# Second half of a two-layer backbone on five token blocks of one column group each, in place of four of two groups

## The chip, the cores and the metric

The kernel runs on one core of a Trainium2 chip. The metric is the device time of one execution in microseconds; the kernel before takes 1913.91 us (median of three runs, 1911.35 to 1915.99). The engines are named as in the profile: PE (TensorE, matrix products), ACT (ScalarE), DVE (VectorE), POOL (GpSimd), and SP, whose queue issues every data transfer (DMA) of this kernel in program order.

## The reference

One step of a two-layer network on 128 prompt tokens and 2048 latent tokens, 2176 in all, with 1024 channels. Layer 0 joins gated linear attention with a spatial gating unit; layer 1 joins a pooling mixer with a short gated convolution. The part that the change touches:

```python
def mix_odd(z, j):                       # layer 1; z = h @ w_in_odd, six parts of 512 channels
    xc, gc, xd, bd, cd, gd = split_cols(z, ODD_SPLITS)
    pooled = concat([centred_mean(xc[..., group i], w) for i, w in enumerate((2, 4, 8, 16))]) - xc
    pooled = einsum('btgc,gcd->btgd', pooled by group, w_pool[j])
    o_c = pooled * pool_scale[j] * silu(gc)
    u = cd * xd
    y = u[t-1] * w_conv[j, 0] + u[t] * w_conv[j, 1] + u[t+1] * w_conv[j, 2]
    return concat([o_c, bd * y * silu(gd)])
# each layer: h = rmsnorm(x) * (1 + scale) + shift;  out = mix(h @ w_in) @ w_out;  x = x + gate * out
# after both layers: y = rmsnorm(x, final_norm_g)
```

## The kernel before, in words

Channels lie on the 128 partitions and tokens along the free axis. Every fp32 product is made of three reduced-precision ones: an operand is split into a high and a low part (`split`, lines 197 to 199: the high part on ACT, the low part on DVE, every third one on POOL), and the product is hi·hi + hi·lo + lo·hi. With 8 contraction tiles of 128 that is 24 matmuls for one tile of 128 output channels and one column group.

The first half of the program is the in-projection of layer 0 with its attention and gating unit. It works on blocks of its own (`BLK`) and its tables are the same in both kernels. The second half works on the token blocks `BLK2`, from the last tokens to the first, because the backward attention state arrives in that order. For each block there are 40 output-channel tiles: 8 of `out0` (out-projection of layer 0), 24 of `in1` (in-projection of layer 1, four heads of six), and 8 of `out1` (out-projection of layer 1). The blocks are interleaved: out0 of the last two blocks, and then, for each block, its in1 and out1 and the out0 of the block two before it. The last block has only in1 and out1 (`out1_last`) left.

`gemm_ch` makes one output-channel tile. It loads the weights anew for every block (`load_w`: one DMA of 512 KB at line 206 into one of `NRAW = 2` raw buffers, then the split into one of three hi and three lo buffers), and runs 24 matmuls for each column group:

```python
for a, b in _groups(c1 - c0):
    pt = gtile()
    o = pt[:, 0:b - a]
    mm3(o, [...])          # 24 matmuls, line 217
    yield a, b, o
tick()
```

`_groups` keeps up to 512 columns in one group and halves what is wider, so a block of 544 gives two groups of 272. A raw weight buffer is free for the next DMA when the low part has been made from it.

Between two blocks the normed input h of in1 is made by `make_t` (line 350) and `make_h` (lines 365 and 366) from x, which is read back tile by tile through two `xk` buffers (line 1018). The tiles of h lie in the same ring as the outputs `ys` of out1, which have to be scaled (line 1126) and stored (line 1128) first; the norm for that is a side thread that runs two channel tiles later (`after(fin, 2)`). For block 1 alone `ys` lies in the `oB` buffers, which out0 of block 0 has just used (the loads into them are line 954). The attention's backward part (`finish_o`, lines 830 to 890) is another side thread, advanced by `tick`. The order of instructions on each engine is fixed when the program is built.

Of the kernel before, what the change touches and what calls it, by code (L numbers as in the profile page):

```python
# [10 lines left out]
F32 = mybir.dt.float32  # L11
# [14 lines left out]
# token ranges of the blocks of layer 0's in-projection; the prompt comes last  # L26
# [3 lines left out]
BLK2 = [(0, 544), (544, 1088), (1088, 1632), (1632, 2176)]  # L30
# [4 lines left out]
W2 = 552  # L35
TMAX = 600
# [44 lines left out]
def kernel(ctx: ExitStack, tc: tile.TileContext, xT, cT, w_ada, b_ada, norm_g, final_g,  # L81
# [33 lines left out]
    def mtile():  # L115
        """two psum banks"""
        return ps.tile([P, 2, 512], F32, tag="m", bufs=banks[0])
# [19 lines left out]
    # side threads: generators advanced as the main line of matrix products is emitted  # L137
# [82 lines left out]
    def gemm_ch(src, acts, c0, c1):  # L220
        """One tile of 128 output channels over columns [c0, c1) of the 8 (hi, lo) operand tiles.
        Yields (a, b, psum) per column group, relative to c0."""
# [12 lines left out]
    def newton(ss, scale, shape, nw=None):  # L235
        """ss (psum, sums of squares) -> (m, r0) with 1/sqrt(ss*scale + eps) = (m + 1.5) * r0."""
# [40 lines left out]
    def silu_psum(src, n, eng, pre=None, dst=None):  # L277
        """psum [P, n] -> SBUF silu; pre: per-partition factor."""
# [25 lines left out]
    def adaln(l, part, wtile, step, halves=(0, 2)):  # L304
        """shift (part 0), scale (1) or gate (2) of layer l for both conditionings, in channels
        [512 * halves[0], 512 * halves[1])."""
# [32 lines left out]
    def cond_ranges(t0, t1):  # L339
        """(a, b, cond) pieces, relative to t0, of tokens [t0, t1)."""  # L340
        out = []
        if t0 < NP:
            out.append((0, min(t1, NP) - t0, 0))
        if t1 > NP:
            out.append((max(t0, NP) - t0, t1 - t0, 1))
        return out
# [33 lines left out]
    # ================= phase 1: layer 0 in-projection, GLA within tiles, SGU =================  # L380
    sg = pool("sg", stack=s1)

    def cols(bi):
        """(column, token, count) of the pieces of block bi"""
        c = 0
        for a, b in BLK[bi]:
            yield c, a, b - a
            c += b - a
# [4 lines left out]
    def prep_x(bi, rr=None):  # L393
        """loads block bi of x and scales it by its norm"""
# [55 lines left out]
    # [hi, 1, 1 | lo | hi] of the low-rank gates against [hi, bias hi, bias lo | hi | lo] of w_gk  # L450
# [22 lines left out]
    def diag_ap(Z, arr, s):  # L473
        """[p, half, block, s]: array arr on first halves, array arr + 1 on second halves."""
# [5 lines left out]
    def gla_tile(t, qk, v, lrT):  # L480
        """GLA of tile t (0: prompt): within the tile in both directions, forward state, and what
        the backward sweep needs."""
# [6 lines left out]
        Z = gl.tile([P, 4, 256], F32, tag="Z", bufs=2)     # Sb, Pf, Sf, Pb  # L489
# [7 lines left out]
        Q1 = gl.tile([P, 2, 2, P], F32, tag="Q1", bufs=2)   # q, level-1 q  # L497
# [6 lines left out]
        while s <= 64:  # L504
# [10 lines left out]
            # advance the prefix and suffix sums to blocks of 2s  # L515
# [10 lines left out]
            if s == 8:  # L526
                # levels of blocks up to 16: 32x32 products, masked and summed
# [26 lines left out]
        # upper levels, laid out as the tile's matrix  # L554
# [23 lines left out]
        # whole-tile factors: backward q, forward q, forward k, backward k  # L578
# [16 lines left out]
        # k factors to token-major, chunk states  # L595
# [6 lines left out]
        # outputs of the tile  # L602
# [36 lines left out]
    def gemm_tok(src, ncol, h, nt):  # L639
        """Token-major: yields (tile, psum[tok, ncol]) for nt tiles of 128 tokens."""  # L640
# [22 lines left out]
    def first_units(h, nt, tok0, qk0):  # L663
        """lr | v and the first products of q, by halves of the contraction, the first half as soon
        as its part of h is there"""
# [16 lines left out]
    def block1(bi):  # L682
# [51 lines left out]
        # spatial gating unit: token-major values, mixed over the 128 positions of a tile  # L734
# [43 lines left out]
    # ================= backward sweep of GLA, norm and gate =================  # L778
# [7 lines left out]
    def open_late():  # L786
# [3 lines left out]
        f3.append(fin_o(3, 1, PER3))  # L790
# [8 lines left out]
    def heads(ap):  # L799
        """[(r k), pr, c] of DRAM as [k, pr, r, c]"""  # L800
# [10 lines left out]
    def states(t):  # L811
        """states entering tile t: [forward | backward, k] x head x v"""
# [16 lines left out]
    def finish_o(bi):  # L829
        """adds the backward state's part, norm and gate of GLA; operands of out-projection 0"""  # L830
# [61 lines left out]
    def fin_o(bi, every, per=1):  # L892
        """finish_o as a side thread; the operands are complete when `out` runs"""
# [38 lines left out]
    # ================= layer 0 out-projection, layer 1 =================  # L932
# [7 lines left out]
    width[:] = [TMAX, 560, 7, 2]  # L940
# [6 lines left out]
    def out_proj(l, t0, t1, o8, res, ytile, done, part=None):  # L947
        """res(c) + gate * (o @ w_out)[c] to done(c, .); returns the sum of squares over channels,
        or calls part with that of all channels but the last, for each column group of the last"""
# [17 lines left out]
    def out0(bi, o8):  # L967
# [6 lines left out]
        def fin():  # L974
            r = tmp.tile([P, 560], F32, tag="r2", bufs=1)[:, 0:n]
# [7 lines left out]
    def range1(bi):  # L983
        """tokens whose layer-1 output block bi makes"""
# [9 lines left out]
    def in1(bi):  # L994
        """layer-1 in-projection and branches; yields after each channel group, then the operands"""
# [17 lines left out]
        r = tmp.tile([P, 560], F32, tag="r", bufs=1)[:, 0:w]  # L1013
# [281 lines left out]
```

## Time and profile before

| | |
|---|---|
| median of three runs | 1913.91 us |
| span of the profiled execution, first to last instruction | 1907.3 us |
| what lies around the span (median less span) | 6.6 us |
| PE busy | 1800.5 us, 94% |
| DVE, ACT, POOL busy | 60%, 45%, 38% |
| second half | from about 859 us to the end |

The profile shows one execution. "x24" is a count of instructions, "idle before" is the time that an engine stood still ahead of them, with what ended it. In a row of matmuls the duration of one is longer than the distance to the next, because they are pipelined: what a matmul costs is read from the distance of the start times. PEclk is the granted clock of TensorE, 1.00 at 2.4 GHz and 0.5 at 1.2 GHz.

### The profile page before, as it was taken

What the parts mean: (1) busy time and instruction counts of PE and PEld (TensorE: products, weight loads), DVE (VectorE), ACT (ScalarE), POOL (GpSimd) and SP (SyncE); (2) the same over time, 40 slices, a digit from 0 to 9 for tenths busy, and PEclk for the clock granted to TensorE, in tenths of its full rate; (3) what the DMA queues carried; (4) which work ended last, traced back from release to release, by engine and by line L of the source; (5) the groups of instructions that cost most, each with busy time, mean ns of one, the idle gap of its engine ahead of it and who ended that gap; (6) DMA issues with size and microseconds to landing.
All of it is one profiled execution on the core that took longest, in us unless ns stands there. A gap on an engine that the chain in (4) does not pass through costs nothing. (4 is left out here: it accounts for less than half of the span.)

```text
span 1907.3 us, 40156 instructions
## 1 busy us (share of the span) xinstructions
PE 1800.5 (94%) x16303; PEld 1673.9 (88%) x16303; DVE 1150.2 (60%) x2069; ACT 858.5 (45%) x1678; POOL 725.4 (38%) x707
## 2 busy tenths in 40 slices
PE   5998899989998999988999999999999999999996
PEld 4886787777787898888899999999999999999996
DVE  5477835875489359766757554775535644636344
ACT  4454645455455356443535442354433433433332
POOL 0423532444153223453534533344533423442343
PEclk9999999999999999998999999999999999999998
DMA  9343424343523342455764343753245622343221
GB/s 321 114 137 117 162 90 151 122 147 119 170 90 113 109 136 81 129 160 170 243 211 156 113 134 114 235 165 111 84 136 177 214 89 89 115 136 128 85 86 63
DMA packets 136122, 263.44 MB, mean 138 GB/s; under 512 B 24192, under 2 KB 60160, under 8 KB 135936
## 3 DMA queue, kind: packets, MB, share of 16 engines
q1 hardware_dynamic: 135936, 260.87, 42.2%
q8 instruction: 128, 2.10, 0.4%
q14 instruction: 58, 0.48, 0.1%
HBM read 219.97 MB, written 40.84 MB: 137 GB/s over the span
## 5 line engine op out<-in xcount | busy, mean ns | idle before, releaser
L217 PE MATMUL ps_g<-ring_hh,wp_hi 128*128 128x272 f32 (+5 forms) x2168 | 679.0, 313 | 9.3 <-DVE tmp_ev L765 5.6
L217 PE MATMUL ps_g<-ring_hh,wp_lo 128*128 128x272 f32 (+5 forms) x2168 | 673.4, 311 | 0.2 <-POOL wp_lo L199 0.2
L217 PE MATMUL ps_g<-ring_hl,wp_hi 128*128 128x272 f32 (+5 forms) x2168 | 671.7, 310 | 1.7 <-DVE ring_hl L366 1.7
L198 ACT ACTIVATE wp_hi<-wp_raw 128x1024 fp32r<-128x1024 f32 (+1 forms) x256 | 270.9, 1059 | 426.3 <-PE ps_g L217 297.1
L217 PEld LDWEIGHTS ps_g<-ring_hh,wp_hi 128*128 128x128 f32 x2168 | 409.7, 189 | 32.7 <-DVE tmp_ev L765 6.6
L217 PEld LDWEIGHTS ps_g<-ring_hl,wp_hi 128*128 128x128 f32 x2168 | 410.2, 189 | 18.3 <-DVE ring_hl L366 2.3
L217 PEld LDWEIGHTS ps_g<-ring_hh,wp_lo 128*128 128x128 f32 x2168 | 409.6, 189 | 16.5 <-POOL wp_lo L199 0.3
L199 DVE TENSOR_TENSOR wp_lo<-wp_raw,wp_hi 128x1024 fp32r<-128x1024 f32 (+1 forms) x175 | 229.5, 1313 | 213.7 <-ACT wp_hi L198 213.2
L199 POOL TENSOR_TENSOR wp_lo<-wp_raw,wp_hi 128x1024 fp32r<-128x1024 f32 (+1 forms) x81 | 198.6, 2452 | 373.5 <-ACT wp_hi L198 373.2
L270 POOL TENSOR_TENSOR tmp_acc<-tmp_acc,tmp_px 128x544 f32<-128x544 f32 (+4 forms) x76 | 120.4, 1584 | 165.7 <-ACT tmp_px L269 162.8
L217 PE MATMUL ps_g<-wp_hi,ring_hh 128*128 128x256 f32 (+1 forms) x528 | 156.1, 298 | 15.0 <-ACT gl_v L700 4.2
L217 PE MATMUL ps_g<-wp_lo,ring_hh 128*128 128x256 f32 (+1 forms) x528 | 152.6, 290 | 1.8 <-POOL wp_lo L199 1.1
L217 PE MATMUL ps_g<-wp_hi,ring_hl 128*128 128x256 f32 (+1 forms) x528 | 152.0, 290 | 1.8 <-DVE ring_hl L366 1.7
L217 PE MATMUL ps_g<-oA_oh,wp_hi 128*128 128x272 f32 (+1 forms) x512 | 148.8, 295 | 4.9 <-ACT oA_oh L198 3.7
L217 PE MATMUL ps_g<-oA_ol,wp_hi 128*128 128x272 f32 (+1 forms) x512 | 149.4, 293 | 2.2 <-DVE oA_ol L199 2.0
L217 PE MATMUL ps_g<-oA_oh,wp_lo 128*128 128x272 f32 (+1 forms) x512 | 149.5, 293 | 0.5 <-DVE wp_lo L199 0.5
L217 PE MATMUL ps_g<-oB_ol,wp_hi 128*128 128x272 f32 (+1 forms) x512 | 147.4, 288 | 1.4 <-POOL oB_ol L199 1.4
L524 POOL TENSOR_TENSOR gl_Z<-gl_Z 128x128 f32<-128x128 f32 x170 | 89.8, 548 | 151.9 <-DVE gl_Z L524 110.5
L217 PE MATMUL ps_g<-oB_oh,wp_hi 128*128 128x272 f32 (+1 forms) x512 | 147.1, 289 | 0.4 <-ACT oB_oh L198 0.4
L217 PE MATMUL ps_g<-oB_oh,wp_lo 128*128 128x272 f32 (+1 forms) x512 | 147.5, 289 | 0.0
L508 ACT ACTIVATE gl_L<-gl_Z 128x256 f32<-128x256 f32 x204 | 82.1, 418 | 90.3 <-DVE gl_Z L524 60.5
L217 PEld LDWEIGHTS ps_g<-wp_hi,ring_hh 128*128 128x128 f32 x528 | 100.5, 191 | 23.0 <-ACT gl_v L700 4.9
(241 smaller groups left out, 3162.6 us busy)
## 6 DMA issues: line engine op xcount, KB each, us to landing
wp_raw<-in_w_dram SPq DMA_DIRECT2D x96, 512.0 KB, 3.6
wp_raw<-in_w0c_dram SPq DMA_DIRECT2D x64, 512.0 KB, 3.8
wp_raw<-in_wo_dram SPq DMA_DIRECT2D x64, 512.0 KB, 3.6
wp_raw<-in_w_ada_dram SPq DMA_DIRECT2D x32, 512.0 KB, 3.6
wp_raw<-in_w0t_dram SPq DMA_DIRECT2D x16, 544.0 KB, 3.5
xs_y<-in_xT_dram SPq DMA_DIRECT2D x32, 272.0 KB, 3.5
dr_x<-xs_y SPq DMA_DIRECT2D x32, 272.0 KB, 3.5
ring_xk<-in_xT_dram SPq DMA_DIRECT2D x32, 256.0 KB, 4.7
```

The source lines that it names most:

```text
L198: act(out=hi, in_=src, func=AF.Copy)
L199: (eng or lo_engine()).tensor_tensor(out=lo, in0=src, in1=hi.bitcast(F32), op=ALU.subtract)
L217: mm(out=out, lhsT=a, rhs=b, start=start and i == 0, stop=stop and i == n - 1)
L270: eng.tensor_tensor(out=acc, in0=acc, in1=sq, op=ALU.add)
L508: act(out=dst.rearrange("p (b t s) -> p t b s", t=2, s=s), in_=diag_ap(Z, 2 * i, s), func=AF.Exp, scale=1.0 / 16.0)
L524: (dve if i >= 2 or s < 4 else gps).tensor_tensor(out=dst, in0=dst, in1=bc(src), op=ALU.add)
```

## The change

The second half works on five blocks, in token order 256, 384, 512, 512 and 512 wide, and the last tokens again come first. Each gives one column group (504 to 512, 384, or 256 to 264 columns). Widths of tiles follow, and the six written-out calls at the end become a loop with the same interleaving.

```diff
-BLK2 = [(0, 544), (544, 1088), (1088, 1632), (1632, 2176)]
+BLK2 = [(0, 256), (256, 640), (640, 1152), (1152, 1664), (1664, 2176)]
-W2 = 552
-TMAX = 600
+W2 = 528
+TMAX = 536
-        f3.append(fin_o(3, 1, PER3))
+        f3.append(fin_o(NB2 - 1, 1, PER3))
-    width[:] = [TMAX, 560, 7, 2]
+    width[:] = [TMAX, 528, 7, 2]
-    g2 = fin_o(2, 1, PER2)
-    out0(3, o3)
-    out0(2, g2())
-    f = fin_o(1, 2)
-    out1(3, run(in1(3), 4))
-    out0(1, f())
-    f = fin_o(0, 2)
-    out1(2, run(in1(2), 4))
-    out0(0, f())
-    out1(1, run(in1(1), 4))
+    last = NB2 - 1
+    f = fin_o(last - 1, 1, PER2)
+    out0(last, o3)
+    out0(last - 1, f())
+    for bi in range(last, 0, -1):
+        if bi > 1:
+            f = fin_o(bi - 2, 2)
+        out1(bi, run(in1(bi), 4))
+        if bi > 1:
+            out0(bi - 2, f())
     o0 = run(in1(0), 4)
```

On PE, out0 of the block with the first tokens. Before, the six rows on the two sides of the border between the two column groups of one channel tile; the weights (`wp_hi_17666`, `wp_lo_17667`) are the same on both sides:

```order
L217 MATMUL ps_g_17670<-oB_oh_17283,wp_hi_17666 128x272
L217 MATMUL ps_g_17670<-oB_ol_17284,wp_hi_17666 128x272
L217 MATMUL ps_g_17670<-oB_oh_17283,wp_lo_17667 128x272
L217 MATMUL ps_g_17697<-oB_oh_14936,wp_hi_17666 128x272
L217 MATMUL ps_g_17697<-oB_ol_14937,wp_hi_17666 128x272
L217 MATMUL ps_g_17697<-oB_oh_14936,wp_lo_17667 128x272
```

Now, the same place: after 24 matmuls of 256 columns the next channel tile comes, with weights of its own.

```order
L217 MATMUL ps_g_16542<-oB_oh_16379,wp_hi_16538 128x256
L217 MATMUL ps_g_16542<-oB_ol_16380,wp_hi_16538 128x256
L217 MATMUL ps_g_16542<-oB_oh_16379,wp_lo_16539 128x256
L217 MATMUL ps_g_16581<-oB_oh_15053,wp_hi_16577 128x256
L217 MATMUL ps_g_16581<-oB_ol_15054,wp_hi_16577 128x256
L217 MATMUL ps_g_16581<-oB_oh_15053,wp_lo_16578 128x256
```

The weights of a channel tile serve 24 matmuls in place of 48. In the whole second half 7680 matmuls of line 217 become 4800, and 160 loads of weights become 200.

On SP, while out0 of block 0 runs and h of block 1 is made. Before, the loads of x for h (`ring_xk`), the stores of out0 (`dr_x`), weights (`wp_raw`), and at the end the first load into an `oB` buffer, which waits for PE:

```order
L1018 DMA ring_xk_17873<-dr_x_2_80_179 128x560
L1018 DMA ring_xk_17880<-dr_x_3_81_180 128x560
L954 DMA xs_y_17792<-in_xT_dram 128x544
L972 DMA dr_x_4_82_181<-xs_y_17597 128x544
L206 DMA wp_raw_17976<-in_w_dram 128x1024
L972 DMA dr_x_5_83_182<-xs_y_17662 128x544
L1018 DMA ring_xk_17887<-dr_x_4_82_181 128x560
L206 DMA wp_raw_18075<-in_w_dram 128x1024
L1018 DMA ring_xk_17894<-dr_x_5_83_182 128x560
L972 DMA dr_x_6_84_183<-xs_y_17727 128x544
L1018 DMA ring_xk_17901<-dr_x_6_84_183 128x560
L954 DMA oB_ol_19624<-dr_x_1_79_178 128x544
```

Now, the same stretch, from the first load into an `oB` buffer on:

```order
L954 DMA oB_ol_17778<-dr_x_1_79_178 128x384
L1128 DMA out_dram<-ring_hl_16324 128x512
L972 DMA dr_x_4_82_181<-xs_y_16573 128x256
L206 DMA wp_raw_16822<-in_w_dram 128x1024
L206 DMA wp_raw_16879<-in_w_dram 128x1024
L954 DMA oB_oh_17743<-dr_x_0_78_177 128x384
L972 DMA dr_x_5_83_182<-xs_y_16612 128x256
L1018 DMA ring_xk_16745<-dr_x_2_80_179 128x400
L1018 DMA ring_xk_16752<-dr_x_3_81_180 128x400
L972 DMA dr_x_6_84_183<-xs_y_16651 128x256
L954 DMA oB_oh_17815<-dr_x_2_80_179 128x384
L954 DMA oB_ol_17852<-dr_x_3_81_180 128x384
```

Of the loads of x only the eighth stood behind the load into `oB` before; now the third to the eighth stand behind it.

On DVE, in1 of block 0 (the last block made), the second head. Before, from one low part of weights (line 199) to the next:

```order
L199 TENSOR_TENSOR wp_lo_21033<-wp_raw_21030,wp_hi_21032 128x1024
L1081 SCALAR_TENSOR_TENSOR tmp_ev_20876<-tmp_ev_20874,tmp_ev_20809 128x128
L1088 TENSOR_TENSOR tmp_ed_20878<-tmp_ev_20874,xs_edge_10417 128x2
L1088 TENSOR_TENSOR tmp_ed_20881<-tmp_ev_20874,xs_edge_10417 128x1
L1081 SCALAR_TENSOR_TENSOR tmp_ev_20876<-tmp_ev_20874,tmp_ev_20809 128x424
L280 TENSOR_SCALAR tmp_ev_20888<-ps_g_20895 128x276
L1090 TENSOR_TENSOR tmp_ev_20876<-tmp_ed_20878,tmp_ev_20809 128x2
L1090 TENSOR_TENSOR tmp_ev_20876<-tmp_ed_20881,tmp_ev_20809 128x1
L280 TENSOR_SCALAR tmp_ev_20888<-ps_g_20926 128x276
L1088 TENSOR_TENSOR tmp_ed_20885<-tmp_ev_20874,xs_edge_10417 128x2
L1090 TENSOR_TENSOR tmp_ev_20876<-tmp_ed_20885,tmp_ev_20809 128x2
L199 TENSOR_TENSOR wp_lo_21094<-wp_raw_21091,wp_hi_21093 128x1024
```

Now, the same stage of the same head:

```order
L199 TENSOR_TENSOR wp_lo_18614<-wp_raw_18611,wp_hi_18613 128x1024
L1081 SCALAR_TENSOR_TENSOR tmp_ev_18554<-tmp_ev_18552,tmp_ev_18513 128x128
L1088 TENSOR_TENSOR tmp_ed_18556<-tmp_ev_18552,xs_edge_10370 128x2
L1088 TENSOR_TENSOR tmp_ed_18559<-tmp_ev_18552,xs_edge_10370 128x1
L1081 SCALAR_TENSOR_TENSOR tmp_ev_18554<-tmp_ev_18552,tmp_ev_18513 128x136
L280 TENSOR_SCALAR tmp_ev_18566<-ps_g_18573 128x264
L1090 TENSOR_TENSOR tmp_ev_18554<-tmp_ed_18556,tmp_ev_18513 128x2
L1090 TENSOR_TENSOR tmp_ev_18554<-tmp_ed_18559,tmp_ev_18513 128x1
L199 TENSOR_TENSOR wp_lo_18651<-wp_raw_18648,wp_hi_18650 128x1024
L1088 TENSOR_TENSOR tmp_ed_18563<-tmp_ev_18552,xs_edge_10370 128x2
L199 TENSOR_TENSOR wp_lo_18686<-wp_raw_18683,wp_hi_18685 128x1024
```

The low parts of the weights keep their 1024 columns and stand closer together among the others, whose widths fall from up to 424 to 136 and from 276 to 264.

## Rows read from the trace of the kernel before

**Rows 1.** The page: span, and busy time of each engine.
```profile
span 1907.3 us, 40156 instructions
PE 1800.5 (94%) x16303; PEld 1673.9 (88%) x16303; DVE 1150.2 (60%) x2069; ACT 858.5 (45%) x1678; POOL 725.4 (38%) x707
```
**Rows 2.** Stretches of block 0: PE, PEld, DVE, ACT, POOL, clock, DMA.
```profile
1697.00:1842.00 145.00, 144.10 (x1131) 143.19 (x1130) 71.05 (x137) 54.53 (x104) 52.51 (x54) 1.00 0.33 107
1842.00:1890.00 48.00, 48.00 (x379) 47.91 (x378) 20.47 (x35) 11.31 (x16) 14.47 (x8) 1.00 0.14 45
```
**Rows 3.** PE's waits, 960 to 1890 us, the first: total, times, longest.
```profile
PE ps_g L217 <- ACT ring_hh L365: 2.8, 5, 1.2
```
**Rows 4.** PE by time, second half (start, duration): 49 steps of 272.
```profile
1443.83 0.29 PE L217 MATMUL ps_g<-oB_ol,wp_hi 128*128 128x272 f32 x1
...
1449.96 0.29 PE L217 MATMUL ps_g<-oB_oh,wp_lo 128*128 128x272 f32 x1
```
**Rows 5.** PE, first half: 16 steps of 512, 16 of 384, 19 of 256.
```profile
435.96 0.39 PE L217 MATMUL ps_g<-ring_hh,wp_lo 128*128 128x512 f32 x1
...
439.60 0.39 PE L217 MATMUL ps_g<-ring_hh,wp_hi 128*128 128x512 f32 x1
...
629.05 0.33 PE L217 MATMUL ps_g<-ring_hh,wp_hi 128*128 128x384 f32 x1
...
631.82 0.33 PE L217 MATMUL ps_g<-ring_hl,wp_hi 128*128 128x384 f32 x1
...
634.09 0.28 PE L217 MATMUL ps_g<-ring_hh,wp_hi 128*128 128x256 f32 x1
...
636.37 0.28 PE L217 MATMUL ps_g<-ring_hl,wp_hi 128*128 128x256 f32 x1
```
**Rows 6.** DVE by time, the end of the program.
```profile
1890.53 0.51 DVE L957 SCALAR_TENSOR_TENSOR yo_y<-ps_g,cst_ada,yo_y 128x276 f32<-128x276 f32 x1 [2.86 <-PE ps_g L217]
1897.60 0.43 DVE L241 TENSOR_SCALAR tmp_nw<-ps_s 128x276 f32<-128x276 f32 x1
1899.68 3.79 DVE L1157 SCALAR_TENSOR_TENSOR yo_y<-yo_y,cst_fg,tmp_nw 128x276 f32<-128x276 f32 x5
```
**Rows 7.** PE by time, start of the second half: two longest waits.
```profile
858.85 0.82 PE L217 MATMUL ps_g<-oA_oh,wp_hi 128*128 128x272 f32 x2 [3.72 <-ACT oA_oh L198]
878.71 0.79 PE L248 MATMUL ps_s<-tmp_px,cst_ones_r 128*128 128x512 f32 x1 [2.62 <-ACT tmp_px L198]
```
**Rows 8.** Tile wp_raw, 1700:1760: ns min/median/max, first and last start.
```profile
L206 SPq DMA_DIRECT2D wp_raw<-in_w_dram x10: 327/328/340, 1700.4 to 1756.2; - x10
L198 ACT ACTIVATE wp_hi<-wp_raw x10: 1042/1062/1062, 1702.9 to 1759.9; 128x1024 fp32r<-128x1024 f32 x10
L199 DVE TENSOR_TENSOR wp_lo<-wp_raw,wp_hi x6: 1211/1226/1227, 1704.0 to 1754.9; 128x1024 fp32r<-128x1024 f32 x6
DMA to landing us min/median/max: 3.4/3.5/3.7
```
**Rows 9.** Groups by line and form, in1 of block 0, 1697:1842.
```profile
L199 DVE TENSOR_TENSOR wp_lo<-wp_raw,wp_hi 128x1024 fp32r<-128x1024 f32 x14 | 17.1, 1223 | 33.9 <-ACT wp_hi L198 33.9
L199 POOL TENSOR_TENSOR wp_lo<-wp_raw,wp_hi 128x1024 fp32r<-128x1024 f32 x9 | 22.1, 2458 | 37.9 <-ACT wp_hi L198 37.9
```
**Rows 10.** POOL and DVE by time, in1 of block 0.
```profile
1742.96 2.39 POOL L199 TENSOR_TENSOR wp_lo<-wp_raw,wp_hi 128x1024 fp32r<-128x1024 f32 x1 [15.54 <-ACT wp_hi L198]
1742.99 3.51 DVE L1055 SCALAR_TENSOR_TENSOR tmp_ev<-tmp_ev,xs_wcv,tmp_ev 128x424 f32<-128x424 f32 x2
```
**Rows 11.** DMA issues: KB each, median us to landing.
```profile
ring_xk<-dr_x SPq DMA_DIRECT2D x24, 280.0 KB, 3.4
```
**Rows 12.** Groups by line and form, 900:1895: low part of h.
```profile
L366 DVE SCALAR_TENSOR_TENSOR ring_hl<-ring_xk,cst_ada,ring_hh 128x432 fp32r<-128x432 f32 x8 | 5.3, 665 | 0.4 <-ACT ring_hh L365 0.4
```
**Rows 13.** SP by time, from out0 of block 0 to in1.
```profile
1473.35 3.18 SPq L1018 DMA_DIRECT2D ring_xk<-dr_x  x2
1487.61 1.43 SPq L954 DMA_DIRECT2D oB_ol<-dr_x  x1
```

More of the change, by code (lines that the diff above doesn't have):

```diff
@@ L974, in fin @@
         def fin():
-            r = tmp.tile([P, 560], F32, tag="r2", bufs=1)[:, 0:n]
+            r = tmp.tile([P, 528], F32, tag="r2", bufs=1)[:, 0:n]
             finish_rstd(acc, n, r)
@@ L1012, in in1 @@
             pads = [(w, bw)] if last else []
-        r = tmp.tile([P, 560], F32, tag="r", bufs=1)[:, 0:w]
+        r = tmp.tile([P, 528], F32, tag="r", bufs=1)[:, 0:w]
         load(out=r, in_=d_r[:, c0:c1])
@@ L1122, in fin @@
         def fin():
-            r = tmp.tile([P, 560], F32, tag="r2", bufs=1)[:, 0:n]
+            r = tmp.tile([P, 528], F32, tag="r2", bufs=1)[:, 0:n]
             finish_rstd(acc, n, r)
```

## The prediction

> **What bounds the kernel now.** Read the engines' busy time first [rows 1]: PE is busy for 94% of the span, DVE for 60%, the others less. The table by stretch [rows 2] then shows that in the second half PE is not only the busiest engine but the bound: 144.1 of 145 us in in1 of block 0 and 48.0 of 48 us in its out1, at a granted clock of 1.00, the upper level (2.4 GHz). The waits say the same: from 960 to 1890 us the largest item in PE's list is 2.8 us in all [rows 3]. So whatever shortens PE's work there shortens the program, until something else is late. Where that can happen is seen in three places: the chain from a raw weight buffer back to the same buffer [rows 8], the instructions of DVE and POOL that hold each other up [rows 9, 10], and SP's queue between two blocks [rows 11 to 13].
>
> The sum is made against the profiled execution, 1907.3 us; 6.6 us lie around it to the median of 1913.91.
>
> **1. Matmuls, -31 us.** Columns are neither added nor removed: 2176 for each of 40 channel tiles and 24 passes. What falls away is the part of a matmul that doesn't depend on its columns, 7680 - 4800 = 2880 times. In the second half 49 steps of 272 columns take 6.13 us, 125.1 ns each [rows 4]; 272 columns at 2.4 GHz are 113.3, so the fixed part is 11.8 ns. In the first half 512 columns take 227.5 ns, 384 take 173.1 and 256 take 120.0 [rows 5], fixed parts of 14.2, 13.1 and 13.3. Before: 7680 x 125.1 = 960.8. After, with the prices of the first half: 2880 x 227.5 + 960 x 173.1 + 960 x 120.0 = 936.6, a gain of 24; with 11.8 for all: 4800 x 11.8 against 7680 x 11.8, a gain of 34. I take 31, nearer to the price of the same stage. Range -24 to -34.
>
> The Trainium skill (TensorE: Matmul & The Clock Gate, section Back-to-back issue gap) gives a warm matmul its columns at 2.4 GHz and about 2.5 ns. By that rule 2880 fixed parts are worth 7 us and the whole sum comes out near 1928; the trace shows 11.8 to 14.2 and decides.
>
> **2. The tail, -5.4 us.** The final norm of the last block follows its last product by column group. Now the second group's sum reaches DVE at 1890.53, its norm has to wait for DVE's five multiplications of the first group until 1897.60, and its own end at 1903.47; the span closes at 1907.3 [rows 6], 16.8 us after the last product. With one group of 264 columns the first wait is gone: two evacuations, a square, two sums and the rsqrt are about 3.8 us (1890.53 to the first group's norm, worked out as 1899.68 - 1897.60 = 2.1 for the rsqrt and 1.7 ahead of it), then 3.8 for the multiplications and 3.8 for the store: 11.4. Range -3 to -6.
>
> **3. Start of the second half, -2 us.** A block of 544 cuts 128-token tiles; 20 pieces of `finish_o` become 17, each with a few products and two sums on PE. PE's first wait there, 3.72 us, and the one of 2.62 [rows 7] come from the operands of out0's last contraction tiles. Ahead of them now lie 21 matmuls each of three channel tiles of 512 columns (14.3 us) in place of 21 each of four groups of 272 (10.5 us), which covers a part. Range -5 to +3.
>
> **4. Weights in the block of 256, +21 us.** Each channel tile needs 24 x 120.0 = 2.88 us of PE at 256 columns and 2.96 at 264, in the mean 2.92; before, one load of weights served 6.0 us. Forty more loads, splits on ACT and low parts on DVE or POOL are issued; in the blocks of 512 (5.46 us a tile) and 384 (4.15) they lie beside the products. At 256 there are two raw buffers, and a buffer comes back only after its whole chain. Rows 8 show one: DMA issued at 1756.2, high part begun at 1759.9, 1.06 long, then the low part, 1.23 on DVE or 2.46 on POOL [rows 9]: 6.1 or 7.3 us, in the mean 6.5, so two buffers give a tile every 3.25 us when nobody waits. That is the lower bound: (3.25 - 2.92) x 40 = 13, less about 4 that the five tiles already on chip lend at the two starts of the stretch: 9.
>
> The upper bound comes from waiting at each step. DVE's instruction of line 1055 begins 0.03 us after a low part on POOL and, two together, lasts 3.51 us [rows 10]: POOL ends at 1745.35, and only 1.15 us of the 3.51 lie behind that. So instructions of these two engines exclude each other. In in1 of block 0 the 24 low parts cost 16 x 1.22 + 8 x 2.46 = 39 us whatever the columns; the rest of POOL, 52.5 - 22.1 = 30.4, falls to 15, and the rest of DVE, 71.1 - 17.1 = 54, to some 27, of which between none and all is of the kind that waits. That makes 54 to 81 us of a resource that PE leaves 24 x 2.92 = 70 for; before it was 70 to 124 of 145. A chain that waits a whole low part on POOL once and an evacuation or two on ACT and DVE is 8.5 us, 4.25 a tile, and (4.25 - 2.92) x 40 - 4 = 49. I take 3.55 a tile, nearer to the lower end, because the low parts' means in rows 9 (1.22 and 2.46) are still close to their least: 0.63 x 40 - 4 = 21.
>
> The Trainium skill (SBUF — State Buffer, section Who interferes with whom) states what rows 10 show: a DVE instruction with two SBUF inputs and a GpSimd one that reads SBUF exclude each other for the whole instruction. By this rule, which the trace bears out, the chain waits and the sum is mine; if the engines ran freely the tile would take 3.25 us and the sum be 1891.5.
>
> **5. Between out0 of block 0 and in1 of block 1, +6 us.** SP issues in order. The first load into an `oB` buffer waits until PE begins out0's eighth tile, since that buffer is its operand. Before it was issued at 1487.61, with only the last load of x behind it; the loads of x had begun at 1473.35 [rows 13]. Now six loads of x stand behind it, and out0 is short. Count from out0's start: the eighth tile begins at 7 x 2.92 = 20.4, with weights a little late 22; two and a half us of other issues, then three pairs of loads through two buffers, each pair 3.4 for landing [rows 11], two DVE passes of 0.67 [rows 12] and an ACT pass of about 0.6 between: 5.3. The last two tiles of h are there at 22 + 2.5 + 16 = 40.5. PE has ended out0 at 25 and can run three channel tiles interleaved over h as it arrives, 12.5 us, of which 3.1 remain behind the last pair: it ends at 43.5 in place of 37.5. I take 6; 0 if the loads get ahead, 12 if the pairs take two microseconds more each among the eight loads into `oB`.
>
> **6. Other transitions and the block of 384, +1 us.** 4.15 us a tile is over 3.55 and under 4.25; out0 of the block of 384 lasts 33 us and h is made meanwhile. Range 0 to 6.
>
> Sum: -31 - 5.4 - 2 + 21 + 6 + 1 = -10.4. 1907.3 - 10.4 = 1896.9 for the span, and with 6.6 around it 1903.5 us.
>
> **Rivals.**
> A. *Weights hide.* The tiles already on chip and a shorter chain keep PE fed in the block of 256, and the loads of x get ahead. For it: before, PE's waits name no weights among the longest [rows 3]. Against: even the chain without a wait is 3.25 against 2.92. Time: 1913.9 - 31 - 5.4 - 2 + 3 = 1879 (1875 to 1891). Chance 0.26.
> B. *Weights decide.* The block of 256 runs at the pace of its weight chain, held up by DVE and POOL excluding each other; all else comes as forecast. Terms 1 to 3, 5 and 6 leave a gain of 31, and the 4 us lent make it 35; over 40 tiles that is 0.87, so from 2.92 + 0.87 = 3.8 us a tile on the change loses. At 4.25 it ends at 1913.9 - 31 + 49 = 1932 (1915 to 1940). For it: the 54 to 81 of 70 us. Against: PE's delay also slows the instructions that compete. Chance 0.26.
> C. *The change doesn't give what it says*, because what a matmul takes beyond its columns grows with them, so that 2880 fewer bring nothing. For it: 14.2 ns at 512 columns against 11.8 at 272 [rows 4, 5]. Against: 256 columns have 13.3, more than half of 14.2. Term 1 would be 0 and the time 1903.5 + 31 = 1934.5 (1925 to 1940). Chance 0.03. The Trainium skill's 2.5 ns under term 1 would end near here too.
> My forecast, 3.3 to 3.8 us a tile, 1893 to 1914: chance 0.45.
>
> **Numbers.** A measurement of this kernel tells 0.2% from no change: 1910.1 and 1917.7. Faster: all of A, three quarters of the forecast, 0.26 + 0.34 = 0.60. Same: the rest of the forecast and a fifth of B, 0.11 + 0.05 = 0.16. Slower: the rest of B and C, 0.24. The range leaves out the lowest of A and the highest of B: 1877 to 1930; the forecast's own is 1893 to 1914.
>
> **What would show it.** Term 1: 4800 matmuls of line 217 in the second half, 512 columns at 226 to 228 ns from start to start. Term 2: one group of norm instructions at the end, 11 to 12 us behind the last product. Term 4: in the last 120 us PE busy for 77 to 88% of the time (2.92 by 3.8 and by 3.3), its waits put down to the high and low parts of weights, and raw buffers' DMAs about 3.55 us apart; over 95% A holds, under 77% B. Term 5: waits for ring_hh and ring_hl at the first tiles of in1 of block 1, 4 to 8 us together. The forecast is wrong if the time gained in the blocks of 512 is not three quarters of term 1, or if PE in the block of 256 waits for evacuations or buffers of PSUM and not for weights.

## The result, and the profile after

The changed kernel takes 1930.04 us (median of four runs, 1927.96 to 1933.06) beside 1912.63 for the kernel before: ratio 1.0094, 95% interval 1.008 to 1.0108. It is slower by some 17 us where a gain of 10 was forecast. Single executions of one kernel lie up to 0.9% apart, so what follows goes by such ratios. (Of the 6.6 us that the table before puts around the span, 1.8 lie around it in one execution, 1927.96 beside a span of 1926.1 here; the rest is that the profiled execution was shorter than the median.) The page of the changed kernel, against [rows 1]:

```profile
span 1926.1 us, 34263 instructions
PE 1800.3 (93%) x13355; PEld 1533.0 (80%) x13355; DVE 1176.2 (61%) x1976; ACT 890.4 (46%) x1608; POOL 779.0 (40%) x741
```

PE has 2948 instructions fewer and is busy for just as long, in a span 18.8 us longer. PE by time shows why fewer matmuls saved so little. Row pairs: 22 steps of 512 columns, and 23 of 256, in the second half (start, duration).

```profile
1299.69 0.40 PE L217 MATMUL ps_g<-ring_hl,wp_hi 128*128 128x512 f32 x1
...
1304.80 0.39 PE L217 MATMUL ps_g<-ring_hh,wp_lo 128*128 128x512 f32 x1
...
1830.26 0.28 PE L217 MATMUL ps_g<-ring_hh,wp_hi 128*128 128x256 f32 x1
...
1832.99 0.28 PE L217 MATMUL ps_g<-ring_hh,wp_lo 128*128 128x256 f32 x1
```

That is 232.3 ns for 512 columns and 118.7 for 256. The means over the unbroken rows of the second half say the same: 232.5 (2193 steps), 175.4 at 384 (912), 118.7 at 256 (435), and 125.7 at 272 in the kernel before (5428). A straight line through them is 4.7 ns and 0.4446 ns a column. So a matmul less is worth 4.7 ns in this half, not 11.8: 2880 of them 13.6 us, not 31. This is the largest miss. (The first half has another price: 512 columns take 227 ns there in both kernels, the median of some 1090 steps, as in [rows 5], and 232 here, the median of 2340.) The rest is in the waits of PE, from the start of in1 to the last product, against a list headed by 2.8 us before [rows 3]:

```profile
PE ps_g L217 <- DVE wp_lo L199: 7.6, 9, 2.9
PE ps_g L217 <- ACT wp_hi L198: 7.0, 9, 1.5
PE ps_s L249 <- DVE tmp_nw L199: 6.8, 2, 4.9
PE ps_g L217 <- DVE xs_y L957: 5.1, 1, 5.1
PE ps_s L1098 <- DVE tmp_ev L1090: 3.5, 2, 2.3
PE ps_g L217 <- ACT ring_hh L365: 2.3, 3, 1.1
PE ps_g L217 <- POOL wp_lo L199: 2.1, 5, 1.0
PE ps_s L1098 <- DVE tmp_ev L1081: 1.7, 1, 1.7
```

Three kinds: weights (16.7 us), extra products that stand between the tiles in PE's queue (12.0), and one evacuation (5.1). By stage, with a stage running to the next one's first product and "matmuls" worked out from the line above:

```
us                        before: stage, matmuls   after: stage, matmuls   rest grows by
first two out0                 121.2     96.6          104.6     89.2          -9.2
last out0 + in1 of block 1     199.1    193.1          143.8    123.9         +13.9
in1 + out1 of block 0          199.8    194.7          115.6     92.7         +17.8
all others                     511.4    481.0          689.8    645.5         +13.9
sum                           1031.5    965.4         1053.8    951.3         +36.4
```

The stages grow by 22.3 us: 14.1 less of matmuls, 36.4 more of all else. The second half starts 1.8 later and the tail is 5.0 shorter, which makes the 18.8 of the span but for rounding. By PE's rows about 27 of the 36.4 us are time in which PE stood still, and about 6 are matmuls at the lower clock level (1.2 GHz): the granted clock is 0.98 from 960 to 1914 us, where it was 1.00 from 960 to 1890.

In the last block, whose rows stand against [rows 2], PE is no longer always busy (PE, PEld, DVE, ACT, POOL, clock, DMA):

```profile
1798.00:1884.00 86.00, 76.36 (x593) 73.82 (x592) 52.77 (x102) 38.99 (x67) 41.29 (x55) 0.98 0.56 173
1884.00:1914.00 30.00, 25.90 (x193) 24.98 (x192) 17.92 (x35) 11.62 (x19) 13.50 (x10) 0.94 0.33 104
```

Its weights, against [rows 8] (ns min/median/max, first and last start): eleven DMAs in 35.2 us are one per 3.52.

```profile
L206 SPq DMA_DIRECT2D wp_raw<-in_w_dram x11: 327/328/328, 1833.8 to 1869.0; - x11
DMA to landing us min/median/max: 3.5/3.7/5.0
```

The longest wait stands between out0 of block 0 and in1 of block 1, in place of what [rows 13] led to. DVE, POOL and PE by time:

```profile
1634.80 7.95 DVE L1126 SCALAR_TENSOR_TENSOR ring_hl<-ring_hl,cst_fg,tmp_r 128x512 f32<-128x512 f32 x8
1642.67 0.60 DVE L957 SCALAR_TENSOR_TENSOR xs_y<-ps_g,cst_ada,xs_y 128x128 f32<-128x128 f32 x2
...
1639.79 2.41 POOL L199 TENSOR_TENSOR wp_lo<-wp_raw,wp_hi 128x1024 fp32r<-128x1024 f32 x1 [4.32 <-ACT wp_hi L198]
...
1637.99 0.28 PE L217 MATMUL ps_g<-oB_ol,wp_hi 128*128 128x256 f32 x1
1643.41 0.66 PE L217 MATMUL ps_g<-ring_hh,wp_hi 128*128 128x384 f32 x1 [5.13 <-DVE xs_y L957]
```

DVE makes the eight multiplications of block 2's final norm in a row; the evacuations of out0's narrow tiles stand behind them, and PE stops until one is done. Two of the 7.95 us are POOL's: six of the eight last 0.74 us, and the eighth, which begins 0.13 us after POOL's low part, 2.83. The other long one is at a row sum of `finish_o` in in1 of block 4:

```profile
984.96 0.69 DVE L1046 TENSOR_TENSOR tmp_ev<-ps_g,tmp_ev 128x512 f32<-128x512 f32 x1
987.25 2.85 DVE L1055 SCALAR_TENSOR_TENSOR tmp_ev<-tmp_ev,xs_wcv,tmp_ev 128x504 f32<-128x504 f32 x1
992.59 0.69 DVE L199 TENSOR_TENSOR tmp_nw<-tmp_px,tmp_px 128x512 fp32r<-128x512 f32 x1
...
988.06 0.40 PE L217 MATMUL ps_g<-ring_hh,wp_hi 128*128 128x512 f32 x1
993.33 0.80 PE L249 MATMUL ps_s<-tmp_nw,cst_ones_r 128*128 128x512 f32 x1 [4.87 <-DVE tmp_nw L199]
993.92 0.63 PE L217 MATMUL ps_g<-ring_hl,wp_hi 128*128 128x512 f32 x1
994.35 0.63 PE L217 MATMUL ps_g<-ring_hh,wp_lo 128*128 128x512 f32 x1
```

The sum's low part waits on DVE behind a tile's evacuation and convolution, PE behind the low part. Afterwards two starts lie 0.43 us apart, at a granted clock of 0.50 (1.2 GHz) from 992 to 998.6 us, so the wait costs a little more than its length. The tail, against [rows 6], has one group:

```profile
1914.31 0.62 DVE L957 SCALAR_TENSOR_TENSOR yo_y<-ps_g,cst_ada,yo_y 128x128 f32<-128x128 f32 x2 [2.17 <-PE ps_g L217]
1916.76 0.43 DVE L241 TENSOR_SCALAR tmp_nw<-ps_s 128x264 f32<-128x264 f32 x1 [1.83 <-ACT tmp_nw L240]
1918.60 3.65 DVE L1157 SCALAR_TENSOR_TENSOR yo_y<-yo_y,cst_fg,tmp_nw 128x264 f32<-128x264 f32 x5
```

### The profile page after: what moved, and what is told of

Read it like the earlier page. It is cut to its first block, busy times and chain, and to the rows that moved or that the text cites. A ratio compares the mean times of both kernels' runs of the same rounds, so it can differ in the third digit from the quotient of the medians.

```text
span 1926.1 us, 34263 instructions
## 1 busy us (share of the span) xinstructions
PE 1800.3 (93%) x13355; PEld 1533.0 (80%) x13355; DVE 1176.2 (61%) x1976; ACT 890.4 (46%) x1608; POOL 779.0 (40%) x741
## 3 DMA queue, kind: packets, MB, share of 16 engines
q1 hardware_dynamic: 140032, 281.92, 46.2%
## 4 chain that ended last, share of the span: by engine, by line
PE 48%; DVE 14%; DMA 9%; ACT 4%; issue 3%; POOL 2%; SPq 1%; DVEq 0%; ACTq 0%; POOLq 0%
PE ps_g L217 44%; DMA wp_raw<-in_w_dram 2%; DVE wp_lo L199 2%; ACT wp_hi L198 2%; DMA ring_xk<-dr_x 2%; DVE ring_xk L350 1%; DVE gl_Z L524 1%; DMA wp_raw<-in_w0t_dram 1%; DVE ring_hl L366 1%; POOL wp_lo L199 1%; DMA wp_raw<-in_wo_dram 1%; SPq L809 1%; PE ps_s L1098 1%; DVE ring_hl L1126 1%; DVE gl_L L513 1%
## 5 line engine op out<-in xcount | busy, mean ns | idle before, releaser
L217 PE MATMUL ps_g<-ring_hh,wp_hi 128*128 128x512 f32 (+3 forms) x1592 | 583.4, 368 | 23.0 <-DVE tmp_ev L765 9.8
L217 PE MATMUL ps_g<-ring_hh,wp_lo 128*128 128x512 f32 (+3 forms) x1592 | 580.6, 365 | 8.1 <-DVE wp_lo L199 7.1
L217 PE MATMUL ps_g<-ring_hl,wp_hi 128*128 128x512 f32 (+3 forms) x1592 | 579.2, 364 | 0.0
L270 POOL TENSOR_TENSOR tmp_acc<-tmp_acc,tmp_px 128x512 f32<-128x512 f32 (+5 forms) x90 | 124.5, 1383 | 132.5 <-ACT tmp_px L269 128.6
L217 PE MATMUL ps_g<-oA_oh,wp_hi 128*128 128x512 f32 (+2 forms) x320 | 123.3, 389 | 5.2 <-ACT wp_hi L198 4.0
L217 PE MATMUL ps_g<-oA_oh,wp_lo 128*128 128x512 f32 (+2 forms) x320 | 124.0, 389 | 1.8 <-DVE wp_lo L199 1.1
L217 PE MATMUL ps_g<-oA_ol,wp_hi 128*128 128x512 f32 (+2 forms) x320 | 124.0, 387 | 0.3 <-POOL oA_ol L199 0.3
L217 PE MATMUL ps_g<-oB_oh,wp_hi 128*128 128x512 f32 (+3 forms) x320 | 109.7, 344 | 1.9 <-ACT wp_hi L198 1.8
L217 PE MATMUL ps_g<-oB_oh,wp_lo 128*128 128x512 f32 (+3 forms) x320 | 109.2, 343 | 1.8 <-POOL wp_lo L199 1.0
L217 PE MATMUL ps_g<-oB_ol,wp_hi 128*128 128x512 f32 (+3 forms) x320 | 108.7, 340 | 0.0
```

The source lines that it names most:

```text
L217: mm(out=out, lhsT=a, rhs=b, start=start and i == 0, stop=stop and i == n - 1)
L270: eng.tensor_tensor(out=acc, in0=acc, in1=sq, op=ALU.add)
```

## The experiments

Times are medians; differences from the changed kernel come from the ratios to the kernel before, times 1912. The 95% interval of such a difference reaches about 4 to 5 us either way, for e6 6. All but e16 start from the changed kernel.

Three theories are weighed in the expectations. T: PE waits in order at many places, behind a tile's single evacuation, at the starts of blocks, and only in part for weights. R1: the weights in the block of 256 are the whole loss. R2: each of the 40 more loads of weights costs PE time wherever it lies.

**The matmuls.** e3 cuts every tile into two groups again, e22 only those of 512:

```diff
-for a, b in _groups(c1 - c0):
+for a, b in [(0, hn), (hn, c1 - c0)]:   # e22: only where c1 - c0 > 400
```

> The changed kernel's five blocks and weight loads, but each tile's product in two column groups again (256+256, 192+192, 128+128): 9600 matmuls in the second half in place of 4800. 4800 fixed parts of 12 us a thousand come back: PE's work by columns and fixed part rises from 936 to about 984 us, +47. T: the evacuations lie inside the tile again and PE is slower, so the excess over that work falls by 20 to 30 us: 1947 to 1957. R1: only what the 0.25 us more a tile cover in the last block, about 10, comes off: 1965 to 1969. R2: the excess stays: 1975 to 1980. If what lies beside the columns does not count per matmul (rival C of the prediction), it stays at 1930.

> The changed kernel's five blocks, with two column groups of 256 (252) only in the three blocks of 512: 4800 + 2880 = 7680 matmuls in the second half, as many as before, no more weight loads than in the changed kernel. If a matmul has a fixed part of 11.8 to 14.2 ns beside columns at 2.4 GHz (term 1 as forecast), 2880 of them bring 34 to 41 us back, less up to 8 of waits that the earlier evacuations take away: 1956 to 1971. If the price is 4.7 ns and 0.4446 ns a column, as the means over all long rows of matmuls say, they bring 13.5, less the same waits: 1936 to 1944.

e3 took 2056.62 (ratio 1.0755, 1.0726 to 1.0783), far outside every expectation, because narrow products have a floor here. 27 steps of 128 columns, 17 of 192:

```profile
1659.98 0.27 PE L217 MATMUL ps_g<-oB_oh,wp_lo 128*128 128x128 f32 x1
...
1662.99 0.28 PE L217 MATMUL ps_g<-oB_oh,wp_lo 128*128 128x128 f32 x1
...
1849.79 0.27 PE L217 MATMUL ps_g<-oA_oh,wp_hi 128*128 128x192 f32 x1
...
1851.68 0.27 PE L217 MATMUL ps_g<-oA_oh,wp_lo 128*128 128x192 f32 x1
```

Both cost 111 ns. With it the work comes out: 960 pairs of 192 at 223 for 175 add 46 us, 960 of 128 at 223 for 120 add 99, 2880 of 256 add 13. That is 158 for the 126 measured, so some 32 us of waits must have gone: PE is then slower than the weights, and its list of waits from 960 us on names no weights. e22 took 1955.77 (1.0225, 1.0211 to 1.0239), +25: neither 13.5 nor, but for its edge, 34 to 41. Its time doesn't decide, since waits grew too: 13.6 more by the price and some 12 beside it. (Most of them in the first two out0 and in in1 of block 3; why is not settled.) Stages without waits decide; out0 of block 2 in the changed kernel, then in e22:

```profile
1161.20:1206.10 44.90, 44.90 (x196) 36.43 (x195) 28.92 (x36) 18.44 (x24) 16.30 (x9) 1.00 0.72 239
```
```profile
1176.00:1222.10 46.10, 46.10 (x388) 46.02 (x387) 32.28 (x43) 18.16 (x24) 16.24 (x9) 1.00 0.72 236
```

192 matmuls more cost 1.2 us, 6 ns each; out1 of blocks 4, 3 and 2 went 46.1 to 46.3, 46.6 to 46.2 and 45.5 to 46.8. Over the four, 768 matmuls cost 2.3 us, 3 ns each; at 11.8 they would have cost 9.1. The steps agree: 256 columns take 118.4 ns in e22 (5063 steps), and twice that is 4.6 more than the 232.1 of 512.

**The weights of the last block.** e4 leaves the low parts out there (`nolo`), e8 adds a third raw buffer in the second half, e12 makes all low parts of the last block on DVE:

```diff
+nolo: act(out=hi, in_=raw); return hi, hi                      # e4
+wp2 = pool("wp2", stack=s2); every third raw tile from it      # e8
-return gps if lo_ctr[0] % 3 == 0 else dve
+return gps if lo_ctr[0] % 3 == 0 and not lodve[0] else dve     # e12
```

> The changed kernel without the low parts of the weights in in1 and out1 of the last block (the high part is multiplied in their place, so the weights there are only their high parts): 32 subtractions of 1.2 us (DVE) or 2.5 us (POOL) are gone, matmuls and DMAs stay. R1: the chain and its wait between DVE and POOL are the loss; excess of those two stages falls from 21.9 to about 8: 1912 to 1917. T: the waits put to low parts (6.3 us) and their share of the others go, the waits for high parts (5.2 us) and for the pooling's operand (2.3) partly stay: 1919 to 1924. R2: under 3 us change, 1927 to 1931.

> The changed kernel with a third raw weight buffer in the second half. The run without low parts took 20 us off the last block's in1 and out1 (115.5 to 95.5 us). Theory a1 (the chain through two raw buffers sets the pace there): three buffers give a tile every 2.2 us in place of 3.25 at best, under PE's 2.92, and 12 to 18 of the 20 us come: 1912 to 1918. Theory a2 (the pace is set by what DVE and POOL have to do and by their holding each other up, 54 to 81 us of 70): a third buffer only lets the queue ahead grow, 0 to 5 us come: 1925 to 1930.

> The changed kernel with every low part of weights and operands in in1 and out1 of the last block on DVE (none on POOL, where one takes 2.4 us against 1.2). Theory a2: a third of the low parts lasts half as long and holds nobody up, some 13 us of a shared resource go, 8 to 14 us come: 1916 to 1922. Theory a1: the chain of those tiles is 1.2 us shorter for one tile in three, 0.2 us a tile in the mean, 5 to 6 us: 1924 to 1926. If DVE itself becomes late (its other work is 27 us beside 39 of low parts in in1's 70): no gain or a loss, 1930 to 1936.

e4: 1910.61 (0.9993, 0.9977 to 1.001), -19 us. Its last block, in1 and out1, has PE busy throughout; in1 lasts 71 us for 85 and out1 25 for 30:

```profile
1801.00:1872.00 71.00, 71.00 (x587) 70.80 (x586) 28.78 (x94) 40.42 (x68) 18.01 (x45) 1.00 0.69 213
1872.00:1897.00 25.00, 24.63 (x199) 24.13 (x198) 8.26 (x23) 10.67 (x18) 5.48 (x7) 1.00 0.33 104
```

The waits for high parts and for the pooling's operand went too, though only low parts were taken out. So the low parts are the cause of that block's whole excess, as R1 said of this block. e8: 1923.88 (1.0052, 1.0033 to 1.0072), -8 us; e12: 1924.26 (1.0059, 1.0038 to 1.008), -7 us. e8 falls between its two expectations. e12 meets the figure for the chain, not that for the shared resource. Its interval reaches into the other's range, so it doesn't tell them apart. A third buffer loosens the way from raw buffer to raw buffer, low parts on DVE shorten it, and either gives a third to two fifths of the 19: no single link holds it. R2 is out: with as many loads of weights, e4 took the whole excess of the last block away.

**Blocks of at least 384.** e1:

```diff
-BLK2 = [(0, 256), (256, 640), (640, 1152), (1152, 1664), (1664, 2176)]
+BLK2 = [(0, 384), (384, 768), (768, 1152), (1152, 1664), (1664, 2176)]
```

> Five blocks of one column group as in the changed kernel, but of 384, 384, 384, 512, 512 tokens, so none is narrower than 384 (4.15 us of PE a weight tile); still 4800 matmuls and 40 more weight loads than before. Theory T (PE waits in order at many places: behind a tile's single evacuation, at the starts of blocks, and only in part for weights in the block of 256): the 14 us of excess in in1 and out1 of the last block go, some 5 of the 13 us at the start of in1 of block 1 go, the longer last block gives 2 back in the tail and the other two blocks of 384 about 2: 1914 to 1918 us against 1930. Rival R1 (weights in the block of 256 are the whole loss): only the stages of the last block change, 1908 to 1912. Rival R2 (each of the 40 more weight loads costs PE time wherever it lies): 1926 to 1932.

1918.29 (1.0027, 1.001 to 1.0044), -13 us: T's upper edge. The last block's excess is gone (in1 105 us, 102 of them matmuls), but in1 of the third block, now 384 wide, carries 24 us beyond its matmuls. The waits move to where tiles are narrow. R1 (1908 to 1912) and R2 (1926 to 1932) both miss.

**PE's order.** e6 puts the row sums of `finish_o` and the pooling's product one weight tile later, and gives the sums' low part a buffer of its own; e16 does this to the kernel before:

```diff
 split(sq, hi, lo)
+yield o8
 sum_rows(ss[:, 0:4 * w], hi, lo)
...
+(pp = stile(); mm(..wpl..); ... split(gx, *o8[hh]))  moved behind the loop over gemm_ch(w1[g + 4], ...)
```

> The changed kernel with two groups of extra products put one tile later in PE's order: the two row sums of finish_o (behind their operand's high and low part) and the pooling's product in in1 (behind the tile of line 1102 in place of ahead of it). T: the waits of PE at these products (tmp_nw 4.9 and 2.0 us, tmp_ev 1.2, 1.7 and 2.3 us, 12 in all) and about 2 us of restarts behind them go: 1915 to 1919. R1 and R2: PE is ahead of the weights, so a wait removed here comes back at the next weight tile: 1926 to 1931.

> The kernel before (four blocks, two column groups) with the two edits of order that were worth 6 us in the changed one: row sums of finish_o and the pooling's product one weight tile later on PE. Theory T (these waits come with one column group a tile, because everything behind a tile's end then waits for its one evacuation): the kernel before has 0.9 us of such waits, so it stays at 1910 to 1913. Rival: the edits shorten any form of the kernel, 1903 to 1907, and the gain of the blocks of 384 with the edits over before is theirs and not the blocks'.

e6: 1923.55 (1.0062, 1.0034 to 1.009), -6 us, half of what was expected: the waits for tmp_nw (6.8 us) are gone from its list, but those for tmp_ev, at the pooling's product, stay (5.4 in all, 5.2 in the changed kernel), and waits for h (4.7 in all) grew. So it is the row sums that it helped. e16: 1908.39 (0.9993, 0.9977 to 1.0008), no change. That the edits undo a loss which the change brought fits both runs, though the 6 us are hardly clear of noise by themselves; e9 below, and the sums of e20 and e21, speak for them too.

**The final norm ahead of out0.** e7 deals the multiplications out (`yield` after each pair), e14 leaves half of them out for one block (`if not (bi == 2 and c % 2)`).

> The changed kernel with the final norm of out1's blocks (eight multiplications of about 1 us on DVE in a row, and their stores) dealt out two at a time over four weight tiles. Theory T: in the changed kernel this row of eight (7.95 us from 1634.80) lies on DVE ahead of the evacuations of out0 of the block of 256, four PSUM tiles of 2.9 us are full, and PE waits 5.1 us; so the excess of out0 of that block falls from 10.6 to about 3 and the kernel gains 5 to 8: 1922 to 1925 us against 1930. Rival S (SP's order, term 5 of the prediction: the loads of x stand behind the loads into oB): the wait moves to ring_hh and ring_hl at the first tiles of in1 of block 1 and under 2 us is won: 1928 to 1931.

> The changed kernel with four of the eight multiplications of the final norm left out for one block (tokens 1152 to 1663; its channels of odd number stay without the norm). The edit that dealt them out left DVE's row of eight where it was, so it tested nothing. Theory T: that row (7.95 us) stands ahead of the evacuations of out0 of the block of 256 and makes PE's wait of 5.1 us; with four it is some 3.9, the wait falls to about 1.2, the excess of that out0 from 10.6 to 6 or 7, and the kernel to 1925 to 1926 us from 1930. Rival S (the order of SP or h arriving late): what is won there is lost at the first tiles of in1 of block 1, 1929 to 1931.

e7: 1930.63 (1.0093), no change, and no test: the scheduler left the row of eight on DVE as it was. e14: 1921.19 (1.005, 1.0032 to 1.0068), -8 us, more than expected. DVE's row and PE's waits from 1615 to 1660 us:

```profile
1636.75 3.10 DVE L1127 SCALAR_TENSOR_TENSOR ring_hl<-ring_hl,cst_fg,tmp_r 128x512 f32<-128x512 f32 x4
1640.91 1.11 DVE L957 SCALAR_TENSOR_TENSOR xs_y<-ps_g,cst_ada,xs_y 128x128 f32<-128x128 f32 x4
```
```profile
PE ps_g L217 <- ACT wp_hi L198: 6.8, 2, 4.3
```

The wait for the evacuation is gone; one for a weight stands there, so out0 of block 0 gains only 1.6 us (29.3 for 31.0), and in1 of block 1 gains 5.8 (107.0 for 112.8), without the waits for a row sum and for h that it had. S's forecast, that what is won there is lost at in1, is refuted. T's is not met either: the gain came behind out0 and not in it. And SP's queue is not cleared: the load of that weight was issued at 1636.94 us, 4.7 behind the one before, with stores of out0 and a load for it between them.

**Do the causes add up?** e20 takes e4, e6 and e14 together; e21 is e6, e8 and e12, with nothing left out.

> The changed kernel with the three edits together that won 20, 8 and 6 us alone: the last block's weights without their low parts, four of eight multiplications of one block's final norm left out, and the two edits of order. If the causes are separate, 34 us go: 1894 to 1898 against 1930, faster than before by 0.8%. If a wait that goes comes back at the next weight tile (40 more loads cost by themselves), 1902 to 1908.

> The changed kernel's blocks with the two edits of order, a third raw weight buffer, and all low parts of the last block on DVE; nothing is left out. Alone the three won 6, 8 and 7 us by their ratios to before. Separate: 1909 to 1912. The buffer and DVE's low parts both shorten the same chain: together 10 at most, 1914 to 1918.

e20: 1896.35 (0.9924, 0.99 to 0.9948), -33 us, as the sum says: the three causes are separate, as far as an interval of 5 us tells. e21: 1909.21 (0.9984, 0.9968 to 0.9999), -21 us, again the sum; its last block takes 98 us for 116.

**Which version is best.** e9: e1's blocks with e6's and e7's edits (e7's again leaves the rows of eight on DVE whole). e11: the same with a third raw buffer, without e7's. e5: blocks of 448 and four of 432 with the edits. e18: blocks of 512, 512, 384, 384, 384 from the first token on, with e6's edits.

> Blocks of 384, 384, 384, 512, 512 together with three edits of order: the row sums of finish_o and the pooling's product one weight tile later on PE, and the final norm dealt out over four tiles. T: from 1918 of the blocks alone the waits at these products go (tmp_nw and tmp_ev together some 12 us between 1190 and 1560 there, with restarts), and some 3 at out0: 1902 to 1908, faster than before by 0.2 to 0.6%. If the blocks' 40 more weight loads or the shorter out0 ahead of each in1 are the cause and not PE's order, these waits come back as waits for weights and h: 1914 to 1919.

> Blocks of 384, 384, 384, 512, 512 with the two edits of order and a third raw weight buffer in the second half. With the blocks and the edits alone it was 1908.3, and waits for high and low parts of weights of 8.6 us were left in its trace. If these are held by the two raw buffers, 4 to 7 of them go: 1901 to 1904. If they are held by what ACT, DVE and POOL have to do at the starts of the blocks, 1907 to 1909.

> Five nearly equal blocks (448, 432, 432, 432, 432) of one column group with the edits of order; no tile is shorter than 4.64 us. Theory T: the narrowest stage decides how much cover the transitions have, so equal blocks lose less there than 384: 1900 to 1906 less what blocks that cut the 128-token tiles cost at finish_o (four more pieces, 3 to 4 us): 1903 to 1909. Rival (transitions cost by their number, not by width): 1908 to 1914, the pieces on top.

> One column group, blocks of 512, 512, 384, 384, 384 with the narrow ones first in the order of execution and the two of 512 last, and the two edits of order. If width beside finish_o's work decides (the narrow blocks then run while finish_o's products and DVE's work for the next block lie beside them), it is slower than with the narrow blocks last (1908): 1912 to 1920. If only the place at the end counts, the last block's excess goes and it is 1902 to 1907; the tail is 3 us longer in both.

e9: 1908.28 (0.9971, 0.9957 to 0.9986): at the upper edge of T, faster than both kernels, by 0.3% and 1.2%; beside e16, which has the edits and not the blocks, it is 4 us, with an interval of 4 either way. e11: 1908.63 (0.9987, 0.9974 to 0.9999): beside e9, the third buffer gives nothing at 384 columns. e5: 1910.2 (0.9995, 0.9982 to 1.0007), between both theories. e18: 1927.44 (1.009, 1.0069 to 1.011), slower than both of its theories allow. It is no clean test of place, because with its halo its last block is 520 wide and falls into two groups of 260; but the loss lies elsewhere. In1 of its three blocks of 384, now first, takes 121, 120 and 110 us for about 101 of matmuls, where e9's take 118, 107 and 105, as the first theory has it.

## Why the prediction was wrong

**Term 1 failed: -31 forecast, -14 measured.** The step is "272 columns at 2.4 GHz are 113.3, so the fixed part is 11.8 ns", with the prices of the first half beside it. In the first half the reading holds: 256, 384 and 512 columns take 120, 173 and 227 ns there (medians), 13 to 14 ns beyond columns at 2.4 GHz at every width, so [rows 5] were typical of it. The 2880 matmuls fall away in the second half, and there that part grows with the columns: it is 11.9 ns at 256, 12.4 at 272, 15.4 at 384 and 19.2 at 512. The prediction took a price at 512 columns over from the first half, and the part at 272 as fixed. The kernel before had no product of 512 columns of line 217 in its second half; its only steps of that width there, seven between row sums, have a median of 235 ns and could have warned. Why the halves differ, at the same granted clock of 1.00, is open. Rival C, with a chance of 0.03, had this mechanism, and a little more than half of its size. With -14 the forecast's other terms come to 1920.5, slower.

The Trainium skill (TensorE: Matmul & The Clock Gate, section Back-to-back issue gap) gives, for a matmul by itself, 2.5 ns beside the columns. The prediction set this aside for the row's 11.8; the 4.7 measured in the second half is much nearer to the page, though its price of a column (2.4 GHz) is not what these rows show, and the first half's 13 ns are not near it. That the prediction's sum by the page, 1928, lies close to the measured 1930 is luck, for terms 3, 5 and 6 missed too.

**Term 2 was right:** -5.4 and -5.0. **Term 3** had the right sign and was too small: -2 against -9.2 in the first two out0 and +1.8 in the start, -7.4 together, outside its range.

**Term 4 was right, in mechanism and nearly in size:** +21 forecast for 40 tiles, +17.8 measured for 32 of them (out0's eight stand in the row of term 5), 19 given back by e4. In1 and out1 of block 0 take 115.6 / 32 = 3.61 us a tile where 3.55 was said; PE is busy for 88% of 1796 to 1914. Rival B's time came, but not by B: the block stayed under 3.8 us a tile.

**Term 5, +6 forecast, +13.9 measured:** the place was right and the cause, for the most part, wrong. PE waits there for evacuations behind DVE's eight multiplications, which is a sign that the prediction named for being wrong; for ring_hh it waits 1.6 us, where 4 to 8 for h were forecast. e14 shows the multiplications to be worth 8 us, most of it in in1. The prediction counted what is queued on SP and not on DVE. How much of the rest is SP's order stays open.

**Term 6 failed: +1 forecast, +13.9 measured.** It priced transitions by whether h is ready and weights keep up. It did not ask what one column group does to PE's own queue: all of a tile's evacuation now falls at the tile's end, and a row sum or a pooling product placed there waits for it on DVE. For the row sums e6 and e16 together bear this out, at some 6 us; for the pooling's product the waits are seen (5.2 us in the list) and e6 left them. The other 8 are not settled, waits for weights and operands at the starts of the blocks and the lower clock level behind them among them. Nor is e20's distance from what terms 1 to 3 alone would give (1912.6 - 14 - 5 - 7.4 = 1886 against 1896).

The Trainium skill (SBUF — State Buffer, section Who interferes with whom) has a DVE instruction with two SBUF inputs and a GpSimd one that reads SBUF exclude each other. The trace agrees: line 1055 takes 2.85 us beside a low part on POOL and 0.74 without one. That this sets the pace of the block of 256, as the upper bound of term 4 had it, no run shows: e12 gave little more than the shorter chain alone explains.

## What to carry to other kernels

Fit the price of a matmul over several widths, from many steps and in the stage where the matmuls will run, before a count of matmuls is turned into time; one width and a nominal clock gave a false fixed part here, and another stage's price at the same width was 2% off, 5 us in this sum for every thousand wide matmuls. When fewer and larger groups are made, list what stands behind each group's end in the order of PE and DVE, for all of a tile's evacuation now lies there. A narrow block pays for its weights as much as a wide one, and here a version with no block under 384 columns and with PE's extra products one tile later was the one that won, by 0.3%.

## What the runs showed of the hardware

In the second half, with a new weight tile for each matmul, 128 and 192 columns cost the same 111 ns (e3); from 252 columns on (116.7 ns, e22) the price follows the line. At the same granted clock of 1.00 the first half's price is another, 120 ns at 256 columns and 227 at 512. Why a column costs 0.4446 ns in the one and about 1/2.4 in the other is open. A DVE instruction of 512 columns with two tensors in SBUF as inputs (line 1126) lasts 0.74 us with POOL idle and 2.83 beside a low part of weights on POOL; one of the same width that reads one of its two from PSUM (line 957) lasts 0.75 us either way.
